# A hybrid decoder step on one core: GpSimd in written order, GpSimd roundings in the first products, later squares, and ACT copies that empty two PSUM banks ahead of the norm

## The chip, the cores and the metric

One core of one Trainium2 chip. The metric is the device time of one execution in microseconds (us); lower is better.

## The reference

One inference step of a one-layer decoder over 560 tokens: 16 meta tokens, 512 prompt tokens and 8 running sequences with 4 new tokens each. All arithmetic is fp32.

```python
def swiglu(x, w_gate, w_up, w_down):
    return (jax.nn.silu(x @ w_gate) * (x @ w_up)) @ w_down

x = x + 0.5 * swiglu(rmsnorm(x, g_ff1), w_ff1_gate, w_ff1_up, w_ff1_down)   # 1024 -> 2816 -> 1024
# mixer on rmsnorm(x, g_mix): q, k, v, o, two gates (4 heads x 128), and two 512-channel inputs
#   mLSTM: chunked, with state C (128 x 128), n, m of each head
#   RG-LRU: causal conv of width 4, block-diagonal gates (8 blocks of 64), linear recurrence h = a h + b
x = x + concat(mlstm_heads, lru_channels) @ w_out                           # 1024 -> 1024
x = x + 0.5 * swiglu(rmsnorm(x, g_ff2), w_ff2_gate, w_ff2_up, w_ff2_down)
y = rmsnorm(x, g_final)
```

(The order of the steps is abridged.) Outputs are y, the states C, n, m of the mLSTM, h of the RG-LRU, and the last conv inputs, for the prompt and for each of the 8 sequences.

## The kernel before

Everything is transposed: channels lie on the 128 partitions, tokens along the free dimension. x is eight tiles of 128 x 560 (`X`), the FFN's hidden size 22 tiles. TensorE (PE) gets fp32 accuracy by pieces: each operand is split into a rounded part `hi` and a remainder `lo`, and a product is the sum of hi·hi, hi·lo and lo·hi (`split_mm`, L296), each in two halves of 280 tokens (272 where the meta tokens are left out). Of weights, ACT rounds `whi` (L259) and VectorE (DVE) subtracts `wlo` (L264), units of 128 x 512 at a time, through rotating buffers of six, running ahead of their use by `AHEAD = 8, 6, 5, 4` units for load, sums, hi and lo. Part of the FFN runs as seven products in place of eight (`product7`, L409; sums of weight blocks are made by DVE in `s`).

PSUM has three double banks (`mm_tile`) and two single ones (`aux_tile`). A product must wait for a bank, so what reads a bank last (an evacuation by DVE or ACT) can hold PE.

The order of the work is written down as lists of short tokens, a step's name and its index. `FF1` and `FF2` are the plain part of the two FFNs, `MID1` and `MID2` the end of their down products mixed with the next norm, `PLAN` is the mixer. The code issues each step's instructions in this order, inside a region in which the engines of `MANUAL` run them as written: PE, ACT and DVE. GpSimd (POOL) and the DMA queue of SP are outside of this set, and a planner orders them by when their inputs come and by their place in the program. The mixer's preamble (`ident`, `cmask`, `smask`, `seqm`, `keep`, `RW`, `ones_r`, L890 to L919, all GpSimd) stands ahead of the region, and the planner places it.

Names that come up below:

- Start of FF1 (L636 to L695): `warm` is 20 matmuls on ones; `wh`, `wl` round and subtract the first weights (both on DVE, L664 and L662); `x`, `l` (`xa xb la lb` for the halves of tile 0) do it for x times the norm's gain (ACT L675, DVE L673); `p` is one 128-channel part of the first gate product (`p0k`) or up product (`p1k`); `s` squares a tile of x on ACT (L687), `a` adds it to `acc` on DVE (L690); `ga`, `gb` are two parts of the next gate product, `pn` the sum of `acc` over the partitions on PE (`psn`, L391), `rs nw` the root, `eg eu` scale a gate or up product by the norm (L544), `u`, `g` are products.
- MID1: `qa` to `qg` are the seven down products of a tile, `ia` to `ig` add them to X (L483).
- PLAN: `v k q x y o` with an index are products of 48 matmuls, `ev ek eq ex` their evacuations. `rg` (`do_wrg`) builds the block-diagonal gate weights: GpSimd memset L925, DMA L927, GpSimd cast L929 and subtraction L930. `g` (`do_g`) is the product for the mLSTM gates; ahead of it GpSimd copies columns of lo into the hi tile (L969), PE then reads them (`pgate`, L972). `ge gf gq ga gb gc gd gp` work on the gates' rows. For an RG-LRU tile `ex` puts the conv's input together (L1115 to L1117), `a` runs the gate matmuls (`prg`, L1145), `cc` makes the coefficients (L1175 on), `cd` sets the sequences' old state (GpSimd L1188), scans (DVE L1190) and copies the last states to `osm` (GpSimd L1191, L1192). For a head, `tk` and `tv` transpose k and v (`pt`, L1297), GpSimd copying a tail first (L1294); `sd` makes GpSimd's sums `D` (L1407 to L1411), `qw` q times weights for the sequences (GpSimd L1418, L1420), `n` the numerator and denominator (`pn`, L1430 to L1454), `cp` the new C states: GpSimd scales the old one by eight instructions (L1512), DVE adds (L1520).
- Tail (L783 to L860): `scale` multiplies the final norm into X and writes y; `state` and `state_out` make the last three heads' prompt states (PE L817, L818; ACT L821, L822).

```python
MANUAL = {mybir.EngineType.PE, mybir.EngineType.Activation, mybir.EngineType.DVE}
PLAN = """
rg1
v0 gn gs0 gs1 g gr0 gr1 ev0 rg0
...
v2 ev2 cd1 hd1 a2 ta2 ca2 b2 cb2 vm1 sk1 qw1 tb2 n1 cc2 cn1 hk2 ce0
```

Of the kernel before, what the change touches and what calls it, by code (L numbers as in the profile page):

```python
# [139 lines left out]
def hymba_step(ctx, tc, xT, wgu1, wdn1, win, wout, wgu2, wdn2, consts, small, c0t, wrg,  # L140
# [507 lines left out]
    for d, w in enumerate((None, (1, 0), (0, 1), (1, 1), (0, 2), (1, 2), None, None)):  # L648
        if d:
            nc.sync.dma_start(X[:, d, :], xT[d])  # L650
        if w:
# [81 lines left out]
    with tc.tile_pool(name="hp2", bufs=1) as hp, tc.tile_pool(name="sp2", bufs=1) as sp:  # L733
# [79 lines left out]
        def state(i):  # L813
            (k, v), t = keys[i], tails[i]
            py = st[:, 129 * i:129 * i + 129]
            for j in range(4):
# [1 line left out]
            pe.matmul(py, t[:, :P], t[:, P:], start=False, stop=True)  # L818
# [4 lines left out]

        fs = range(c0, c1)
        with tc.manual_schedule(engines=MANUAL | {mybir.EngineType.Pool}):
            for d in range(TAIL, KD):
# [33 lines left out]
            nc.scalar.dma_start(o_small[:, O_NP:O_NP + LATER], osm[:, O_NP:O_NP + LATER])  # L860
# [3 lines left out]
def mixer(ctx, tc, e):  # L864
# [318 lines left out]
    @step
    def do_cd(ct):
# [3 lines left out]
        pool.tensor_copy(ti[:, 528:584].rearrange("p (b j) -> p b j", j=7)[:, :, 2], C[:, H0 + 8 * ct:H0 + 8 * ct + 8])  # L1188
# [225 lines left out]
    def do_qw(h):  # L1414
# [5 lines left out]
        pool.tensor_tensor(qn, qw, n0.unsqueeze(2).to_broadcast([P, NB, 4]), op=ALU.mult)  # L1420

    @step
    def do_n(h):
# [29 lines left out]
        pe.matmul(pn[:, 1, 64:96], one_m[1][:32, :], W[:32, WO[5]:WO[5] + 32], start=True, stop=False)  # L1453
# [210 lines left out]
```

## Time and profile before

| | before |
|---|---|
| median of 3 runs | 1024.83 us (1024.37 to 1026.25) |
| profiled execution, its own time | 1024.98 us |
| its span | 1023.3 us |
| PE busy | 1010.1 us (99%) |
| DVE, ACT, POOL busy | 831.6, 558.3, 119.8 us |
| DMA | 102.85 MB, 101 GB/s on the mean |

How to read it: a busy share is of the whole span. Rows of the timeline give start, duration, engine, line, operation, tile out<-in, shape and count; in brackets stands the idle time of the engine before, and what ended it. `x48` means that so many instructions are put together in one row. Rows of the waits are: who waited, for whom, us in total, times, longest. Rows of the chain (start, duration, engine, tile, line) follow the work that ended last. PEld is PE's loading of weights, PEclk the clock that PE was granted (1.00 is full).

### The profile page before, as it was taken

To read this page: it belongs to the slowest core of one execution; us is meant where nothing else is said; L and a number is where in the kernel's file an instruction comes from. 1 tells how busy PE (TensorE), PEld (TensorE's weight loads), DVE (VectorE), ACT (ScalarE), POOL (GpSimd) and SP (SyncE) were. 2 spreads that over 40 slices of the span, in tenths; PEclk is the share of its full clock that TensorE was granted. 3 is DMA by queue.
4 is the path that set the end of the run, shared out by engine and by line. 5 is a ranking of instruction groups with operands and counts; after the bars stand their busy time and mean duration, and the time that the engine had idled before them with its cause. 6 is when DMAs were issued, how large, how long until landed. Compare 5 with 4: busy or idle time off the path is not lost.

```text
span 1023.3 us, 20215 instructions
## 1 busy us (share of the span) xinstructions
PE 1010.1 (99%) x7786; PEld 995.2 (97%) x7786; DVE 831.6 (81%) x1462; ACT 558.3 (55%) x1071; POOL 119.8 (12%) x198
## 2 busy tenths in 40 slices
PE   9999999999999999998999999999999999999998
PEld 8999999999999999998999999999999999999997
DVE  7988788888788797879888865799888899859774
ACT  6544555565544455475756743554555665654543
POOL 0000000000000035353651202100000000000002
PEclk9999999999999999998999999999999999999999
DMA  6222223223332334234142133223323323235222
GB/s 227 95 83 88 99 94 112 85 98 109 89 104 60 102 103 146 86 95 138 54 135 97 62 104 107 73 63 103 109 89 103 104 94 114 93 102 157 78 71 96
DMA packets 60985, 102.85 MB, mean 101 GB/s; under 512 B 8512, under 2 KB 16976, under 8 KB 60888
## 3 DMA queue, kind: packets, MB, share of 16 engines
q1 hardware_dynamic: 60200, 101.23, 30.8%
q8 instruction: 61, 1.00, 0.4%
q10 hardware_dynamic: 688, 0.32, 0.1%
q14 instruction: 36, 0.29, 0.1%
HBM read 95.20 MB, written 6.33 MB: 99 GB/s over the span
## 4 chain that ended last, share of the span: by engine, by line
PE 86%; DVE 7%; issue 2%; ACT 2%; POOL 2%; DMA 1%; SPq 0%; DVEq 0%; ACTq 0%; POOLq 0%
PE pb L409 27%; PE pad L409 20%; PE pd L296 15%; PE po L296 6%; PE pg L296 3%; PE pu L296 3%; PE pv L296 2%; PE py L296 2%; PE pq L296 2%; DVE wlo L264 2%; PE pd L792 1%; POOL c L1512 1%; PE px L296 1%; PE p L296 1%; PE pk L296 1%
## 5 line engine op out<-in xcount | busy, mean ns | idle before, releaser
L259 ACT CAST whi<-raw 128x512 fp32r<-128x512 f32 (+2 forms) x289 | 172.4, 606 | 160.7 <-PE pad L409 41.6
L264 DVE TENSOR_TENSOR wlo<-raw,whi 128x512 fp32r<-128x512 f32 (+2 forms) x289 | 197.2, 699 | 68.2 <-ACT whi L259 65.4
L259 ACT CAST whi<-s 128x512 fp32r<-128x512 f32 x180 | 111.8, 622 | 106.2 <-PE pb L409 36.4
L264 DVE TENSOR_TENSOR wlo<-s,whi 128x512 fp32r<-128x512 f32 x180 | 124.3, 692 | 12.6 <-ACT whi L259 6.5
L409 PE MATMUL pad<-q21h,whi 128*128 128x280 f32 (+1 forms) x360 | 104.2, 290 | 0.9 <-DVE X L483 0.9
L409 PE MATMUL pb<-qt4l,whi 128*128 128x280 f32 (+1 forms) x360 | 104.0, 289 | 0.0
L409 PE MATMUL pad<-q21l,whi 128*128 128x280 f32 (+1 forms) x360 | 104.0, 289 | 0.0
L409 PE MATMUL pad<-q21h,wlo 128*128 128x280 f32 (+1 forms) x360 | 104.0, 289 | 0.0
L409 PE MATMUL pb<-qt4h,whi 128*128 128x280 f32 (+1 forms) x360 | 103.9, 289 | 0.0
L409 PE MATMUL pb<-qt4h,wlo 128*128 128x280 f32 (+1 forms) x360 | 103.9, 289 | 0.0
L409 PEld LDWEIGHTS pad<-q21h,whi 128*128 128x128 f32 x360 | 67.8, 188 | 1.1 <-ACT whi L259 1.1
L409 PEld LDWEIGHTS pb<-qt4h,whi 128*128 128x128 f32 x360 | 67.9, 189 | 0.0
L409 PEld LDWEIGHTS pb<-qt4h,wlo 128*128 128x128 f32 x360 | 67.8, 188 | 0.0
L409 PEld LDWEIGHTS pb<-qt4l,whi 128*128 128x128 f32 x360 | 67.8, 188 | 0.0
L409 PEld LDWEIGHTS pad<-q21l,whi 128*128 128x128 f32 x360 | 67.8, 188 | 0.0
L409 PEld LDWEIGHTS pad<-q21h,wlo 128*128 128x128 f32 x360 | 67.8, 188 | 0.0
L239 DVE TENSOR_TENSOR s<-raw 128x512 f32<-128x512 f32 x90 | 61.5, 684 | 1.8 <-DMA raw<-in_wdn 1.8
L296 PE MATMUL pd<-hh,whi 128*128 128x280 f32 (+1 forms) x294 | 61.3, 290 | 0.6 <-ACT whi L259 0.4
L296 PE MATMUL pd<-hl,whi 128*128 128x280 f32 (+1 forms) x294 | 61.4, 290 | 0.2 <-DVE hl L557 0.2
L296 PE MATMUL pd<-hh,wlo 128*128 128x280 f32 (+1 forms) x294 | 61.2, 289 | 0.0
L378 POOL TENSOR_TENSOR acc<-acc,sq 128x560 f32<-128x560 f32 (+1 forms) x6 | 9.4, 1564 | 419.8 <-ACT sq L377 419.7
L409 PE MATMUL pb<-q11h,whi 128*128 128x280 f32 (+1 forms) x180 | 52.4, 291 | 0.0
(466 smaller groups left out, 2993.9 us busy)
## 6 DMA issues: line engine op xcount, KB each, us to landing
raw<-in_wgu SPq DMA_DIRECT2D x174, 256.0 KB, 2.7
raw<-in_wdn SPq DMA_DIRECT2D x71, 256.0 KB, 2.7
raw<-in_win SPq DMA_DIRECT2D x50, 256.0 KB, 3.3
raw<-in_wout SPq DMA_DIRECT2D x16, 256.0 KB, 3.1
raw<-in_wdn SPq DMA_DIRECT2D x18, 192.0 KB, 2.3
c<-in_c0t SPq DMA_DIRECT2D x4, 512.0 KB
out_o_cs<-c SPq DMA_DIRECT2D x4, 512.0 KB, 3.0
X<-in_xT SPq DMA_DIRECT2D x7, 280.0 KB, 5.0
```

The costliest lines, as they stand in the source:

```text
L239: dve.tensor_tensor(q[k], q[x], q[y], op=op)
L259: act.copy(ready[i][0][:, :src.shape[-1]], src)
L264: dve.tensor_tensor(lo, src, hi, op=ALU.subtract)
L296: state["mm"] = pe.matmul(ps[:, hf, :n], a[:, ws], b[k][:, c0 + hf * n:c0 + hf * n + n], start=first and j == 0 and i == 0, stop=last and ...
L378: (dve if d == KD - 1 else pool).tensor_tensor(self.acc[:, c0:], self.acc[:, c0:], s[:, c0:], op=ALU.add)
L409: pe.matmul(ps, a[:, k * P:k * P + P], b, start=first and k == 0 and i == 0, stop=k == KD // 2 - 1 and i == 2, skip_group_check=not first)
L792: pe.matmul(pd[d - TAIL][:, hf, :b - a], u[:, o:o + P], v[:, C16 + a:C16 + b], start=f == c0 and m == 0, stop=f == c1 - 1 and m == 2)
L1512: pool.tensor_scalar(c0[:, b, :], c0[:, b, :], Wb[:, b, 3:4], None, op0=ALU.mult)
```

## The change

It has six parts.

- GpSimd joins `MANUAL`: its instructions in the regions run as written.
- FF1's start: the constants' first DMA goes from SP's queue to ACT's; the order of loads changes; all roundings `wh` but the first go to GpSimd; `p00` is done by halves (`pa pb`); squares and their adds come later; `ga` takes four tiles instead of three; two ACT copies (`co`) empty the banks of the first two products ahead of the norm, and `eg0 eu0` then scale in SBUF; the weights of `w3` are prepared earlier.
- MID1: `ib3 if3` ahead of `qe3`.
- Mixer: some tokens change place; `cw` (the scaling of the old C) is a step of its own right after `n`; `cc1` is split into `ci1` and `cj1`; several small operations move from GpSimd to DVE (the sum of Wi, xp's memset and copy, a0's and V's memsets, the th copy of `cd`), and `E`'s minimum from DVE to GpSimd; `om` is copied and written in `gq`; `qw` gets a third GpSimd operation that adds a row of W to `qn`, and `n` drops the matmul L1453.
- FF2: for f = 2 the up product's evacuation and pieces run by halves; `rd3` ahead of `yb3`, `rd5` ahead of `d7`.
- Tail: each of the three states has its own bank, and is copied out and written by itself; GpSimd scales two tiles in place of one.

```diff
-MANUAL = {mybir.EngineType.PE, mybir.EngineType.Activation, mybir.EngineType.DVE}
+MANUAL = {mybir.EngineType.Pool, mybir.EngineType.PE, mybir.EngineType.Activation, mybir.EngineType.DVE}
 PLAN = """
 rg1
 v0 gn gs0 gs1 g gr0 gr1 ev0 rg0
...
-q0 ek0 gd ge
-k1 gf L0 eq0 ex0 cx0 gp hq0 hk0 ek1 gq hx0 tv0
+q0 ek0 gd
+k1 eq0 gf ge L0 ex0 cx0 tv0 gp ek1 hq0 hk0 gq hx0
...
-k2 ca1 cb1 ek2 cc1 tv1 am1
-x2 f0 cv1 p0 ex2 cf0 tk1 cp0 cx2 ck1
+k2 ca1 cb1 ek2 ci1 tv1 am1
+x2 f0 cv1 p0 ex2 cf0 tk1 ck1 cp0 cj1 cx2
...
-v2 ev2 cd1 hd1 a2 ta2 ca2 b2 cb2 vm1 sk1 qw1 tb2 n1 cc2 cn1 hk2 ce0
+v2 ev2 cd1 hd1 a2 ta2 ca2 b2 cb2 vm1 sk1 qw1 tb2 n1 cw1 cc2 cn1 hk2 ce0
...
 FF1 = """
-warm wh00 xa0 la0 wl00 xb0 lb0 p00 x1 wh10 wl10 l1 p10 p01 s0 p11 x2 l2 wh01 wl01 s1 p02 x3 l3 wh11 p03 wl11 p12 p13 a1 s2
-x4 wh02 l4 wl02 p04 s3 x5 l5 p05 wh12 wl12 p14 p15 a2 s4 x6 l6 p06 p16 a3 x7 l7 p07 p17 s5 a4 w0 s6 s7 a5 w1 a6 a7 ga1 pn
-w2 rs0 nw0 rs1 nw1 eg0 sg0 ...
+warm wh00 xa0 la0 wl00 xb0 pa0 lb0 pb0 wh10 wl10 p10 x1 l1 p01 p11 x2 l2 wh01 wl01 p02 wh11 wl11 x3 l3 p12 p03 p13 s0
+x4 l4 wh02 wl02 p04 wh12 wl12 x5 l5 p14 p05 p15 s1 x6 l6 p06 p16 s2 x7 l7 p07 p17 s3 a1 w0 s4 a2 s5 a3 w1 s6 a4 s7 co0 co1 a5 a6 a7 ga1 pn
+w2 w3 rs0 nw0 rs1 nw1 eg0 sg0 ...
...
 FF2 = """
-em2 Bh2 Eh2 hh2 hl2 Bl2 tc2 El2 td2 Fh2 d0 ya3 rd0 Ah3 d2 Fl2 Al3 rd2 d3 d4 yb3 d5 Bh3 rd3 rd4 ta3 d1 Bl3 d7 tb3
-rd5 tc3 Eh3 d6 td3 rd1 El3 Fh3 rd6 Fl3 rd7
+ei2 Bh2 Eh2 hi2 hj2 Bl2 tc2 El2 td2 Fh2 d0 ya3 rd0 Ah3 d2 Fl2 Al3 rd2 d3 d4 rd3 yb3 d5 Bh3 rd4 ta3 d1 Bl3 rd5 d7 tb3
+tc3 Eh3 d6 td3 rd1 El3 Fh3 rd6 Fl3 rd7
...
 MID1
-... nq2 nq6 qe3 ib3 if3 ie3 ...
+... nq2 nq6 ib3 if3 qe3 ie3 ...
...
+    act.dma_start(C[:, :8], consts[:, :8])
     act.activation(dum, eps_c, AF.Identity)
...
-            split_mm(ps["g", f], range(3), nrm.hi, nrm.lo, c0, last=False, w=[z["w"]])
+            split_mm(ps["g", f], range(KD // 2), nrm.hi, nrm.lo, c0, last=False, w=[z["w"]])
...
+        def out(j):
+            what = "gu"[j]
+            z[what, 0] = z_tile()[:, c0:]
+            act.copy(halves(z[what, 0], n), start[j][:, :, :n])
...
-                dve.tensor_copy(h[:, o], src)
+                (pool if j or p else dve).tensor_copy(h[:, o], src)
...
     def do_cd(ct):
...
-        pool.tensor_copy(ti[:, 528:584]..., C[:, H0 + 8 * ct:H0 + 8 * ct + 8])
+        dve.tensor_copy(ti[:, 528:584]..., C[:, H0 + 8 * ct:H0 + 8 * ct + 8])
...
         pool.tensor_tensor(qn, qw, n0.unsqueeze(2).to_broadcast([P, NB, 4]), op=ALU.mult)
+        qs = qn.rearrange("p b j -> p (b j)")[:32]
+        pool.tensor_tensor(qs, qs, d["W"][:32, WO[5]:WO[5] + 32], op=ALU.add)
...
-        pe.matmul(pn[:, 1, 64:96], one_m[1][:32, :], W[:32, WO[5]:WO[5] + 32], start=True, stop=False)
-        pe.matmul(pn[:, 1, 64:96], one_m[1], d["qn"].rearrange("p b j -> p (b j)"), start=False, stop=True)
+        pe.matmul(pn[:, 1, 64:96], one_m[1], d["qn"].rearrange("p b j -> p (b j)"), start=True, stop=True)
...
     @step
+    def do_cw(h):
+        c0, Wb = D[h]["c0"], D[h]["Wb"]
+        for b in range(NB):
+            pool.tensor_scalar(c0[:, b, :], c0[:, b, :], Wb[:, b, 3:4], None, op0=ALU.mult)
...
         def state(i):
-            py = st[:, 129 * i:129 * i + 129]
+            py = st[i] = mm_tile("st")[:, 0, :129]
...
+            state_out(0)
             scale(a, b, pool, 7, 8, nc.scalar)
-            for d0, d1 in ((0, 1), (1, 3), (3, 5), (5, 7)):
+            state_out(1)
+            scale(a, b, pool, 6, 7, nc.scalar)
+            for d0, d1 in ((0, 1), (1, 3), (3, 5), (5, 6)):
                 scale(a, b, dve, d0, d1, nc.sync)
-            for i in range(LATER):
-                state_out(i)
-            nc.scalar.dma_start(o_cp[0:LATER].rearrange("h p e -> p h e"), cp)
-            nc.scalar.dma_start(o_small[:, O_NP:O_NP + LATER], osm[:, O_NP:O_NP + LATER])
+            state_out(2)
+            nc.sync.dma_start(o_small[:, O_NP:O_NP + LATER], osm[:, O_NP:O_NP + LATER])
```

More of the change, by code (lines that the diff above doesn't have):

```diff
@@ L49 @@
 q3 cv2 ek3 hx3 eq3 p1 s2 tk2 cp1 cd2 ck2
-v3 qw2 m2 vm2 L3 a3 sd2 hd2 ev3 n2 ta3 ca3 b3 hk3 cb3 cn2 tv3 tb3 cc3 sk2 am3 cd3
+v3 qw2 m2 vm2 L3 a3 sd2 hd2 ev3 n2 cw2 ta3 ca3 b3 hk3 cb3 cn2 tv3 tb3 cc3 sk2 am3 cd3
 o0 p2 hq3 cv3 ce2 ce3 cl2 cl3 cm2 w3 cp2 eo0
@@ L53 @@
 o1 eo1 mo0 s3 my0 m3 f2 sd3
-y1 tk3 cf2 to1 hd3 ey1 gy1 ck3 so0 mo1 n3 sk3 cn3 cm3
+y1 tk3 cf2 to1 hd3 ey1 gy1 ck3 so0 mo1 n3 cw3 sk3 cn3 cm3
 y2 ey2 so1 f3
@@ L77 @@
 FF1 = """
-warm wh00 xa0 la0 wl00 xb0 lb0 p00 x1 wh10 wl10 l1 p10 p01 s0 p11 x2 l2 wh01 wl01 s1 p02 x3 l3 wh11 p03 wl11 p12 p13 a1 s2
-x4 wh02 l4 wl02 p04 s3 x5 l5 p05 wh12 wl12 p14 p15 a2 s4 x6 l6 p06 p16 a3 x7 l7 p07 p17 s5 a4 w0 s6 s7 a5 w1 a6 a7 ga1 pn
-w2 rs0 nw0 rs1 nw1 eg0 sg0 ya0 yb0 Ah0 Bh0 Al0 eu0 ta0 gb1 tb0 mu0 Eh0 Bl0 tc0 td0 eg1 Fh0 Fl0 El0 ya1 yb1 hh0 Ah1 u1 sg1 Bh1 hl0 Al1 eu1 g2 mu1 u2 ta1 Bl1 tb1 hh1 eg2 eu2 tc1 sg2 mu2 hl1 g3 td1 hh2 hl2 eg3 Eh1 sg3 Fh1 El1 mg3 u3 ya2 em3 Ah2 hh3 Fl1 hl3 yb2 d4 Al2 ta2 Bh2 Bl2 tb2 tc2 rd4 d0 d2 Eh2 rd0 td2 Fh2 El2 d6 Fl2 ya3 yb3 rd6 Ah3 Bh3 Bl3 d5 rd2 Al3 ta3 d3 tb3 rd5 d1 Eh3 v2 tc3 El3 td3 Fh3 d7 rd1 v3 Fl3 rd7 rd3
+warm wh00 xa0 la0 wl00 xb0 pa0 lb0 pb0 wh10 wl10 p10 x1 l1 p01 p11 x2 l2 wh01 wl01 p02 wh11 wl11 x3 l3 p12 p03 p13 s0
+x4 l4 wh02 wl02 p04 wh12 wl12 x5 l5 p14 p05 p15 s1 x6 l6 p06 p16 s2 x7 l7 p07 p17 s3 a1 w0 s4 a2 s5 a3 w1 s6 a4 s7 co0 co1 a5 a6 a7 ga1 pn
+w2 w3 rs0 nw0 rs1 nw1 eg0 sg0 ya0 yb0 Ah0 Bh0 Al0 eu0 ta0 gb1 tb0 mu0 Eh0 Bl0 tc0 td0 eg1 Fh0 Fl0 El0 ya1 yb1 hh0 Ah1 u1 sg1 Bh1 hl0 Al1 eu1 g2 mu1 u2 ta1 Bl1 tb1 hh1 eg2 eu2 tc1 sg2 mu2 hl1 g3 td1 hh2 hl2 eg3 Eh1 sg3 Fh1 El1 mg3 u3 ya2 em3 Ah2 hh3 Fl1 hl3 yb2 d4 Al2 ta2 Bh2 Bl2 tb2 tc2 rd4 d0 d2 Eh2 rd0 td2 Fh2 El2 d6 Fl2 ya3 yb3 rd6 Ah3 Bh3 Bl3 d5 rd2 Al3 ta3 d3 tb3 rd5 d1 Eh3 v2 tc3 El3 td3 Fh3 d7 rd1 v3 Fl3 rd7 rd3
 """.split()
@@ L109 @@
 ie1 qf1 id1 ns0 d6 ns1 qa2 e7 ia2 qb2 qc2 rd6 ig1 qd2 ib2 ic2 if2 qa3 ia3 qe2 ie2 qg2 qf2 ig2 re7 qb3 id2 nq1 qc3
-ic3 qd3 nq2 nq6 qe3 ib3 if3 ie3 nq5 qg3 ns5 nq4 ns2 qf3 id3 t7 ns4 ig3 nq3 ns6 ns3 rt7 ns7 nq7
+ic3 qd3 nq2 nq6 ib3 if3 qe3 ie3 nq5 qg3 ns5 nq4 ns2 qf3 id3 t7 ns4 ig3 nq3 ns6 ns3 rt7 ns7 nq7
 """.split()
@@ L538, in em, with ei, hi, hj @@
             tt(halves(z["u", f], n), ps["u", f][:, :, :n], halves(z["g", f], n), op=ALU.mult)
+        def ei(f):
+            z["u", f] = z_tile()[:, c0:]
+            for hf in range(2):
+                o = slice(hf * n, hf * n + n)
+                tt(z["u", f][:, o], ps["u", f][:, hf, :n], z["g", f][:, o], op=ALU.mult)
+        def hi(f):
+            for hf in range(2):
+                o = slice(hf * n, hf * n + n)
+                act.copy(h[f][0][:, c0 + hf * n:c0 + hf * n + n], z["u", f][:, o])
+        def hj(f):
+            for hf in range(2):
+                o, q = slice(hf * n, hf * n + n), slice(c0 + hf * n, c0 + hf * n + n)
+                tt(h[f][1][:, q], z["u", f][:, o], h[f][0][:, q], op=ALU.subtract)
         def scaled(what):
             def fn(f):
+                if (what, f) in z:
+                    tt(z[what, f], z[what, f], r[:, c0:], op=ALU.mult)
+                    return
                 z[what, f] = z_tile()[:, c0:]
-                src = ps[what, f] if (what, f) in ps else start["gu".index(what)]
-                tt(halves(z[what, f], n), src[:, :, :n], halves(r[:, c0:], n), op=ALU.mult)
-            return fn
+                tt(halves(z[what, f], n), ps[what, f][:, :, :n], halves(r[:, c0:], n), op=ALU.mult)
+            return fn
+        def out(j):
+            what = "gu"[j]
+            z[what, 0] = z_tile()[:, c0:]
+            act.copy(halves(z[what, 0], n), start[j][:, :, :n])
         def sg(f):
@@ L607, in rd @@
             return fn
-        steps.update(ga=first_part, gb=second_part, mg=mg, em=em, g=product("g"), u=product("u"), pn=nrm.mean, rs=nrm.table, nw=nrm.step, eg=scaled("g"), eu=scaled("u"), sg=sg, mu=mu,
+        steps.update(ga=first_part, gb=second_part, mg=mg, em=em, co=out, ei=ei, hi=hi, hj=hj, g=product("g"), u=product("u"), pn=nrm.mean, rs=nrm.table, nw=nrm.step, eg=scaled("g"), eu=scaled("u"), sg=sg, mu=mu,
                      hh=hh, hl=hl, ya=y(0), yb=y(1), ta=ta, tb=tb, tc=tc_, td=td, d=dn("d", *plain), rd=rd("d"), v=run_ahead)
@@ L635, in hymba_step @@
     n1.open()
-    nc.sync.dma_start(C[:, :8], consts[:, :8])
     w0, wt = [[raw_tile(), raw_tile()] for _ in range(2)], [[hl_tile(), hl_tile()] for _ in range(2)]
@@ L647, in hymba_step @@
     nc.sync.dma_start(X[:, 0, Q:], xT[0, :, Q:])
[L648 to L651, printed above, removed]
+    load_w(1, 0)
+    for d, *ws in ((1,), (2, (0, 1), (1, 1)), (3,), (4, (0, 2)), (5, (1, 2)), (6,), (7,)):
+        nc.sync.dma_start(X[:, d, :], xT[d])
+        for w in ws:
             load_w(*w)
@@ L676, in start_x, with start_p @@
         return fn
-    def start_p(j, d):
+    def start_p(j, d, hfs=(0, 1)):
         p = start.setdefault(j, None)
@@ L682, in start_p @@
         t = wt[j][d // 4]
-        split_mm(p, [d], n1.hi, n1.lo, 0, d == 0, d == KD - 1, w=[[u[:, d % 4 * P:] for u in t]])
+        split_mm(p, [d], n1.hi, n1.lo, 0, d == 0, d == KD - 1, hfs, w=[[u[:, d % 4 * P:] for u in t]])
     def start_sq(d):
@@ L698, in hymba_step @@
                   xa=start_x(0, Q, 0), la=start_x(0, Q, 1), xb=start_x(Q, T, 0), lb=start_x(Q, T, 1), p=start_p,
+                  pa=lambda d: start_p(0, d, (0,)), pb=lambda d: start_p(0, d, (1,)),
                   s=start_sq, a=start_add, w=up_to)
@@ L820, in state_out @@
         def state_out(i):
-            act.copy(cp[:, i, :], st[:, 129 * i:129 * i + P])
-            act.copy(osm[:, O_NP + i:O_NP + i + 1], st[:, 129 * i + P:129 * i + P + 1])
+            act.copy(cp[:, i, :], st[i][:, :P])
+            act.copy(osm[:, O_NP + i:O_NP + i + 1], st[i][:, P:])
+            nc.scalar.dma_start(o_cp[i], cp[:, i, :])
         fs = range(c0, c1)
@@ L849, in hymba_step @@
             root(1)
-            st = aux_tile("st")
+            st = {}
             cp = tmp("cp")[:, :LATER * P].rearrange("p (a b) -> p a b", b=P)
@@ L1032, in do_ge @@
         Wi, E = mp.tile([H, NB, 4], F32, name="Wi"), row("E")
-        pool.tensor_tensor(Wi, blk4(A[:, NP:T]), m0.unsqueeze(2).to_broadcast([H, NB, 4]), op=ALU.add)
+        dve.tensor_tensor(Wi, blk4(A[:, NP:T]), m0.unsqueeze(2).to_broadcast([H, NB, 4]), op=ALU.add)
         act.activation(E, mrow, AF.Exp, scale=-1.0)
         act.activation(Wi, Wi, AF.Exp)
-        dve.tensor_scalar(E, E, 1e17, None, op0=ALU.min)
+        pool.tensor_scalar(E, E, 1e17, None, op0=ALU.min)
         act.activation(E, E, AF.Square, scale=EPS ** 0.5)
@@ L1092, in do_gq @@
                           seqm.unsqueeze(1).to_broadcast([96, H, NB]), op=ALU.mult)
+        mrow = G["m"]
+        pool.tensor_copy(om[:, 0:1], mrow[:, NP - 1:NP])
+        pool.tensor_copy(om[:, 1:9], seq(mrow, 3))
+        nc.sync.dma_start(e["o_m"], om)
     def bias(i, j, h):
@@ L1111, in do_ex @@
         xp = L[ct]["xp"] = slot("xp")
-        pool.memset(xp[:, 0:3], 0.0)
-        pool.tensor_copy(smp(xp, 0, 3),
+        dve.memset(xp[:, 0:3], 0.0)
+        dve.tensor_copy(smp(xp, 0, 3),
                          C[:, CS + 24 * ct:CS + 24 * ct + 24].rearrange("p (b j) -> p b j", j=3))
@@ L1171, in do_cc, with do_ci @@
     @step
-    def do_cc(ct):
+    def do_ci(ct):
         l = L[ct]
-        tr, ti, a0, tt, xc = l["th", 0], l["th", 1], l["a0"], l["tt"], l["xc"]
+        a0, tt = l["a0"], l["tt"]
         dve.tensor_scalar(a0, a0, 0.5, 0.5, op0=ALU.mult, op1=ALU.add)
@@ L1177, in do_cc, with do_cj @@
         dve.scalar_tensor_tensor(a0, tt, 2.0, a0, op0=ALU.subtract, op1=ALU.mult)
+    @step
+    def do_cj(ct):
+        l = L[ct]
+        tr, ti, a0, xc = l["th", 0], l["th", 1], l["a0"], l["xc"]
         dve.tensor_tensor(tr, tr, a0, op=ALU.mult)
@@ L1180, in do_cc @@
         dve.tensor_scalar(a0, a0, -2.0, -1.0, op0=ALU.mult, op1=ALU.add)
-        pool.memset(a0[:, 528:584].rearrange("p (b j) -> p b j", j=7)[:, :, 2], 0.0)
+        dve.memset(a0[:, 528:584].rearrange("p (b j) -> p b j", j=7)[:, :, 2], 0.0)
+    @step
+    def do_cc(ct):
+        do_ci(ct)
+        do_cj(ct)
     @step
@@ L1310, in do_cv @@
         v5w = mp.tile([96, P], F32, tag="v5w", name="v5w", bufs=1)
-        pool.memset(V[:, :, 128:129], 1.0)
+        dve.memset(V[:, :, 128:129], 1.0)
         act.activation(v5w, pt[:96, 1, 128:256], AF.Identity, scale=wst[:96, 5, h:h + 1])
@@ L1506, in do_cp @@
     @step
+    def do_cw(h):
+        c0, Wb = D[h]["c0"], D[h]["Wb"]
+        for b in range(NB):
+            pool.tensor_scalar(c0[:, b, :], c0[:, b, :], Wb[:, b, 3:4], None, op0=ALU.mult)
+    @step
     def do_cp(h):
@@ L1510, in do_cp @@
         px, py = ps["p", h]
-        for b in range(NB):
-            pool.tensor_scalar(c0[:, b, :], c0[:, b, :], Wb[:, b, 3:4], None, op0=ALU.mult)
         pn = mp.tile([P, 9], F32, tag="cpn", name="cpn", bufs=2)
```

8 lines of the change are left out of this document (2 added, 6 removed).

## The prediction

> **What bounds the kernel now.** I read the page's busy times first, then the waits, then the windows for stages that the change touches.
>
> ```profile
> span 1023.3 us, 20215 instructions
> PE 1010.1 (99%) x7786; PEld 995.2 (97%) x7786; DVE 831.6 (81%) x1462; ACT 558.3 (55%) x1071; POOL 119.8 (12%) x198
> L264 DVE TENSOR_TENSOR wlo<-raw,whi 128x512 fp32r<-128x512 f32 (+2 forms) x289 | 197.2, 699 | 68.2 <-ACT whi L259 65.4
> PE pt L1297 <- DVE xp L1117: 4.0, 1, 4.0
> PE pad L409 <- DVE X L483: 0.9, 1, 0.9
> DVE hs L1190 <- POOL th L1188: 6.3, 4, 4.5
> PE pq L296 <- DVE kT L955: 0.3, 1, 0.3
> PE pl L1209 <- DVE c L1520: 0.3, 1, 0.3
> ```
>
> PE is busy for 1010.1 of 1023.3 us, so only 13.2 us of idle time can be won, besides matmuls removed or run at a low clock. GpSimd (POOL) has 12% of work: its load can't bound anything, its order can. The waits name two PE stalls that the change aims at (columns: us in total, times, longest), 4.0 us at `pt` in the mixer and 0.9 at `pad` in MID1, and one behind them: VectorE's scan waited 4.5 us for a tiny GpSimd copy. The profiled execution took 1024.98, 0.15 above the median of 1024.83; the sum is made against it.
>
> **The start.** Windows (length, then busy time of PE, PEld, DVE, ACT, POOL, then clock, DMA share, GB/s) and timeline rows:
>
> ```profile
> 5.36:20.63 15.27, 14.15 (x98) 13.07 (x98) 13.04 (x24) 12.99 (x20) 0.00 (x0) 1.00 0.81 281
> 20.63:35.24 14.61, 14.38 (x104) 13.48 (x103) 12.58 (x23) 6.54 (x11) 0.00 (x0) 1.00 0.27 88
> 5.36 1.20 PE L296 MATMUL p<-xh,whi 128*128 128x280 f32 x2
> 21.43 1.51 DVE L690 TENSOR_TENSOR acc<-acc,sq 128x560 f32<-128x560 f32 x2
> 22.99 1.21 PE L391 MATMUL psn<-acc,ones 128*128 128x280 f32 x4
> 35.24 6.19 PE pg L296 x48
> 395.25 0.67 POOL L929 CAST wrgh<-wrg 128x512 fp32r<-128x512 f32 x1 [2.35 <-DMA wrg<-in_wrg]
> ```
>
> A product is 48 matmuls in 6.19 us (the chain's row at 35.24), 0.129 each. The first two are 96 of them, 12.4 us, but take 15.27, with VectorE busy for 13.04. The change takes five weight roundings off VectorE (three of 128x256, two of 128x512) and puts them on an empty GpSimd; the 0.67 row is its price for 128x512, and half of that for 128x256 makes 2.4 us in all, beside other work. The first matmul stays at 5.36, behind the warm-up matmuls, which aren't changed; the constants' DMA, moved from SP's queue to ACT's, lets SP's loads begin one issue (some 0.45) earlier and costs ACT an issue before its first rounding, neither of which that start waits for. With VectorE relieved, the earlier loads and the norm's squares after the roundings, the products are limited by the arrival of x and weights: 12.4 and some 1.2 of waits, end near 19.0. `ga` has 24 matmuls now (3.1 us), so the norm's sum comes at about 22.2 (VectorE's last adds, 0.75 each, end at 21.3 to 22.8) where `psn` stood at 22.99. Behind it follow `psn` 0.62, `gb` 24 matmuls 3.1, `u1` 6.2, and 0.4 to 1.0 of waits: end at 32.5 to 33.1, where `g2` began at 35.24. The two ACT copies that empty the banks (12.99 busy before 20.63, 6.54 in the next 14.6) fit in ACT's idle time. VectorE is at 12.58 of 14.61 there and can give back up to 0.5 later. Taken: **−2.1**; bounds 0 (VectorE no faster) and −2.7.
>
> [...]
>
> **MID1: `ib3 if3` ahead of `qe3`.**
>
> ```profile
> 373.06 2.37 DVE L264 TENSOR_TENSOR wlo<-raw,whi 128x512 fp32r<-128x512 f32 x2
> 373.50 3.15 POOL L378 TENSOR_TENSOR acc<-acc,z 128x560 f32<-128x560 f32 x2 [1.27 <-ACT z L377]
> 375.35 0.79 DVE L483 SCALAR_TENSOR_TENSOR X<-pad,X 128x280 f32<-128x280 f32 x2
> 395.37 0.45 DVE L330 SCALAR_TENSOR_TENSOR rn<-psn,r 128x280 f32<-128x280 f32 x1
> ```
>
> PE waits for the bank that L483 reads; that read stands behind two weight subtractions of 2.37 us. Put ahead of them, it frees the bank before PE asks. **−1.0** (the 0.9 wait and its edges; bounds 0 and −1.1).
>
> **GpSimd in written order: the gate product `g`.** GpSimd's rows and the first matmul of `g`:
>
> ```profile
> 382.64 0.98 POOL L969 CAST whi<-wlo 128x160 fp32r<-128x160 f32 x2 [2.23 <-DVE wlo L264]
> 386.10:391.40 5.30, 5.30 (x41) 5.13 (x40) 4.69 (x7) 1.87 (x4) 5.15 (x19) 1.00 0.81 277
> 391.43 0.51 POOL L925 MEMSET wrg<- 128x512 f32 x1
> 396.01 1.45 POOL L930 TENSOR_TENSOR wrgl<-wrg,wrgh 128x512 fp32r<-128x512 f32 x1
> 391.98 0.63 PE L972 MATMUL pgate<-xh,whi 128*128 128x280 f32 x2
> ```
>
> Today the planner lets L969's two copies, which `pgate` reads, run at 382.64, ahead of everything of the mixer. In the order of PLAN, `rg1` is the first token and `g` the sixth. With GpSimd among the engines in written order, L969 stands behind `rg1`'s memset, its cast, which waits for a DMA behind that memset, and its subtraction. That memset came at 391.43, behind the mixer's preamble (5.15 us of GpSimd from 386.10), the cast at 395.25, the subtraction ended at 397.46, and a copy takes 0.49 and some 0.1 to be seen: 398.1 instead of 383.6. PE is ready at 391.98: **a wait of 6.1**. Behind PE in order stand `x0` and everything else. What a wait of this size does to the clock is shown by the mixer's 4.0:
>
> ```profile
> 468.50:472.80 4.30, 0.29 (x3) 0.11 (x3) 4.25 (x10) 0.00 (x0) 0.35 (x3) 0.74 0.22 68
> 472.80:477.00 4.20, 4.20 (x20) 4.11 (x21) 3.37 (x6) 2.12 (x6) 0.78 (x2) 0.50 0.63 201
> 477.00:481.50 4.50, 4.50 (x36) 4.50 (x36) 4.36 (x7) 2.98 (x6) 0.00 (x0) 0.96 0.29 117
> ```
>
> 4.2 us at 0.50 and 4.5 at 0.96 lose 2.1 + 0.2. A 6.1 wait costs this too: 6.1 + 2.1 = **+8.2**. Bounds: 0, if the copies still come first; +2.2, if the memset goes ahead of the preamble (it needs a buffer that GpSimd's own work frees at 386.1): 386.6 memset, cast after DMA and preamble at 391.9, subtraction to 394.1, no clock loss. I take the upper end, because the preamble and the memset start at nearly the same moment and the preamble is earlier in the program.
>
> **The mixer.**
>
> ```profile
> 461.20:490.30 29.10, 25.09 (x179) 24.35 (x177) 26.29 (x41) 15.56 (x35) 11.23 (x20) 0.88 0.39 128
> 461.18 1.38 DVE L1190 TENSOR_TENSOR_SCAN hs<-a,th 128x584 f32<-128x584 f32 x1 [4.52 <-POOL th L1188]
> 487.03 0.69 POOL L1418 TENSOR_TENSOR qw<-qT,Wb 128x32 f32<-128x32 f32 x1
> 490.32 0.74 DVE L953 TENSOR_TENSOR vT<-pv,r 128x560 f32<-128x560 f32 x1 [1.14 <-PE pv L296]
> 492.88 1.53 DVE L1190 TENSOR_TENSOR_SCAN hs<-a,th 128x584 f32<-128x584 f32 x1 [1.15 <-POOL th L1188]
> 496.59 0.40 POOL L1191 COPY osm<-hs 128x1 f32<-128x1 f32 x1
> 491.87 0.34 PE pn L1430 x4
> 497.20 0.24 PE pn L1453 x2
> ```
>
> The copy L1188 goes to VectorE, so the 4.52 us wait at 461.18 is gone, VectorE is some 4.3 us earlier, and the `pt` wait falls to about 0.4: −3.6, and −2.2 with the clock. But `qw1`, at 487.03 today, is written behind `cd1`, whose GpSimd copies L1191 follow the scan, and that follows `ev2` (the 490.32 row). Counted from the end of `v2`: `ev2` 0.15 + 0.74, L1187 0.76, th copy 0.2, scan 1.45, the copies 0.4, then `qw1`'s three small operations, of which the first two are the last that matmuls before L1454 can cover: at least 4.05. PE is ready for `n1` 1.59 after `v2` (`prg`, 490.28 to 491.87): a wait of 2.45 or more. VectorE has 26.29 us of work in the 29.1 up to 490.3, and 0.5 more from GpSimd; with 4.3 of advance and 1.9 of waits left it brings `n1` to start at about 490.3, after some 4.1 of PE idle that takes with 6 chances in 10 the clock loss of 2.1. `n1` then ends at 497.1, where 497.6 was (L1453 at 497.20, then L1454): **−0.5** for the whole stretch (−3.4 if `n1`'s wait is 2.45 at full clock, +0.7 if both are worst). So most of the advance is given back in a new wait of the same size, 20 us later. [...]
>
> Dropping L1453 (its 0.24 and the gap to the next row's start, −0.31 each) in `n2 n3` gives −0.6; in `n0` and `n1` it lies inside a wait or is counted already. The GpSimd sum that replaces it (some 0.5) is inside the 4.05. `ek1` earlier and the new order of `cw`, `cp`: −0.6, the two waits for `kT` and `pl` at 0.3 each. The split of `cc1` takes half of its VectorE chain from ahead of `tv1` to behind `cp0`, where VectorE is 4.3 ahead: 0. The small memsets, Wi's sum, `E`'s minimum and the copies of `om` with their DMA, now issued from `gq` instead of `ge`, feed no matmul within several products (6.2 us each): 0, and SP's queue, past which that DMA moves, holds only weights four to eight units ahead. Mixer: −0.5 −0.6 −0.6 = **−1.7**.
>
> **FF2.**
>
> ```profile
> 694.70 1.35 DVE L505 SCALAR_TENSOR_TENSOR X<-pd,X 128x544 f32<-128x544 f32 x2
> 695.56 0.49 PE L296 MATMUL pd<-hh,whi 128*128 128x272 f32 x2 [0.43 <-ACT whi L259]
> ```
>
> PE stands about 0.6 before 695.56, for a weight prepared behind `yb3`'s sums and `rd3`; `rd3` ahead of `yb3`, `rd5` ahead of `d7` and `f=2` by halves: **−0.8** (0 to −1.0).
>
> **The tail.**
>
> ```profile
> 1018.50 0.48 PE L818 MATMUL st<-kv 16*128 16x129 f32 x2
> 1020.27 0.49 ACTq L860 DMA_DIRECT2D out_o_small<-osm  x1
> out_o_cp<-cp SPq DMA_DIRECT2D x1, 64.0 KB, 2.6
> ```
>
> All three states are copied out after the last matmul (1018.50), and the last DMA is issued at 1020.27. With a bank for each, only one copy and a 64 KB DMA remain; the last issue comes at about 1019.4 (−0.9), but is followed by a transfer of this size, 2.6 to land, where a small one stood; I give 0.3 back: **−0.6** (−1.2 to +0.2).
>
> **Sum:** −2.1 −1.0 +8.2 −1.7 −0.8 −0.6 = +2.0: 1027.0 by the profiled execution, 1026.8 for the median.
>
> **Rivals.** *B, the memset goes ahead of the preamble:* `g` waits 2.2, and 1026.8 − 6.0 = 1020.8. For it: L969 itself overtook the preamble at 382.64. Against: its buffer is free only at 386.1. *C, the written order leaves L969 where it was* (the change doesn't do there what its flag says, or the weights of `rg1` land early enough): 1026.8 − 8.2 = 1018.6. For it: the copies ended at 383.6, 8.4 us before PE needed them, so their inputs allow it. *D, slower: GpSimd's roundings hold VectorE's two-input steps in the first 20 us:* the start's −2.1 is lost, 1028.9; it decides once VectorE loses over 2 us before 21.4. For it: the pair at 373.06 takes 1.2 each beside GpSimd's two-input sum at 373.50, where the group's mean is 0.70 (the L264 row at the top); against: the 0.45 beside the cast, and casts have one input.
>
> **How the numbers follow.** A measurement of this kernel tells about 0.2% (2.0 us) from no change: faster is under 1022.8, slower over 1026.9. My forecast has 0.60, with its own range 1023.5 to 1029 from the bounds of `n1` and the start; it lies at the edge, so 0.06 of that is faster, 0.30 the same, 0.24 slower. B 0.13 (0.12 faster, 0.01 same), C 0.19 (all faster), D 0.08 (slower). Together 0.37, 0.31, 0.32. The range from 1017.0 to 1030.0 leaves out half of C below and little of D above.
>
> **What would show it.** Start: `psn` near 22.2 and `g2` near 33. MID1: no PE wait at `pad`. `g`: PE waits for GpSimd L969 by some 6 us, and a clock of 0.50 in the 4 us behind it. Mixer: no wait at `pt`, a new one of 2.5 to 4 at `n1` for `qn`. If `pgate` follows `psn` without a gap, the forecast is wrong by 8, and the change is faster.

## The result and the profile after

The changed kernel is slower: 1039.2 us (median of 6, 1034.86 to 1042.61) against 1025.07, ratio 1.0134 with a 95% interval of 1.01 to 1.0168. Its six times fall into two groups, 1034.9 to 1036.3 at a mean granted clock of 0.993 and 1042.1 to 1042.6 at 0.984; the profiled execution is one of the first (1034.86, span 1033.1), so its time is 9.9 above that of the profile before. I forecast 1026.8 and 1017 to 1030.

The page's first lines and the PE rows of the waits (who waited, for whom, us, times, longest):

```profile
span 1033.1 us, 20223 instructions
PE 1010.7 (98%) x7778; PEld 996.0 (96%) x7778; DVE 834.4 (81%) x1479; ACT 559.9 (54%) x1074; POOL 126.1 (12%) x188
```

```profile
PE pn L1468 <- POOL qw L1454: 6.2, 1, 6.2
PE pgate L997 <- POOL whi L994: 5.2, 1, 5.2
PE pt L1335 <- POOL t L1330: 2.2, 1, 2.2
PE pv L296 <- DVE xl L368: 1.1, 1, 1.1
PE pl L1245 <- DVE c L1561: 0.8, 1, 0.8
PE pden L1476 <- ACT zh L1300: 0.7, 1, 0.7
```

PE has as much work as before and 9.2 us more of idle time. The `pt` wait of 4.0 for VectorE is gone; three new ones, 13.6 us together, all name GpSimd (POOL), which is busy for 12% of the span. L994 are the copies of `g` (L969 before), L1330 the copy of v's tail (L1294), L1454 is `qw` (L1418).

Where the time came from, by start times of the same matmuls in both traces (PE's lead or lag against before): −2.6 us at `g2` (35.08 before, 32.44 after); −3.7 behind MID1; −2.6 at the norm's `psn` (391.25, 388.61); +2.9 when `pgate` starts and +5.6 at `x0` behind it; +8.5 behind the wait at L1335, +7.5 at `px` of `x1`, +7.0 at the first `prg` and +6.7 behind `n0`; +0.7 at head 1's `pA`, since the old `pt` wait is gone; +7.1 when `n1` starts and +9.2 behind it; +10.5 at FF2; +9.8 at the end.

The windows show the clock (length, then busy time of PE, PEld, DVE, ACT, POOL, then clock, DMA share, GB/s), first of the changed kernel's profile, then of its other group, from the experiment `again`:

```profile
388.60:394.90 6.30, 1.12 (x6) 0.58 (x4) 3.98 (x7) 1.47 (x3) 3.19 (x8) 0.95 0.39 108
394.90:402.00 7.10, 7.07 (x33) 7.07 (x34) 2.69 (x3) 0.62 (x1) 2.83 (x4) 0.56 0.10 22
429.40:434.00 4.60, 4.58 (x35) 4.32 (x36) 3.45 (x8) 2.57 (x8) 3.00 (x7) 1.00 0.23 70
498.80:503.00 4.20, 4.20 (x11) 2.87 (x12) 3.99 (x7) 1.04 (x2) 4.11 (x4) 0.50 0.17 64
503.00:508.00 5.00, 5.00 (x31) 4.02 (x30) 0.11 (x2) 0.95 (x4) 3.67 (x7) 0.95 0.00 0
```

```profile
430.00:436.00 6.00, 6.00 (x36) 5.74 (x35) 5.11 (x10) 2.62 (x8) 2.47 (x5) 0.72 0.15 52
494.00:500.40 6.40, 0.25 (x2) 0.01 (x1) 6.33 (x11) 5.82 (x7) 2.83 (x4) 0.68 0.26 82
500.40:516.00 15.60, 15.55 (x52) 12.49 (x53) 6.06 (x11) 4.56 (x11) 7.79 (x10) 0.50 0.05 17
```

Both groups have the same waits. In the second one the clock is also low behind L1335 (0.72 where it was 1.00), and behind `n1` it stays at 0.50 for some 16 us in place of under 5. Lined up matmul by matmul, that is +1.5 and +5.2 us: nearly all of the 6.9 us between the two profiles.

GpSimd's rows for the three waits, in the changed kernel:

```profile
387.94 0.52 POOL L950 MEMSET wrg<- 128x512 f32 x1
392.35 0.61 POOL L954 CAST wrgh<-wrg 128x512 fp32r<-128x512 f32 x1 [2.93 <-DMA wrg<-in_wrg]
393.05 1.34 POOL L955 TENSOR_TENSOR wrgl<-wrg,wrgh 128x512 fp32r<-128x512 f32 x1
394.34 1.02 POOL L994 CAST whi<-wlo 128x160 fp32r<-128x160 f32 x2
427.27 1.61 POOL L1061 TENSOR_SCALAR E<-E 4x560 f32<-4x560 f32 x1 [6.00 <-ACT E L1059]
429.11 0.26 POOL L1330 COPY t<-vT 128x96 f32<-128x96 f32 x1
496.37 0.56 POOL L1227 COPY osm<-hs 128x1 f32<-128x1 f32 x1 [3.56 <-DVE hs L1226]
496.87 1.20 POOL L1228 COPY osm<-hs 128x8 f32<-128x8 f32 x1
498.04 0.69 POOL L1454 TENSOR_TENSOR qw<-qT,Wb 128x32 f32<-128x32 f32 x1
```

Each time the engine stands idle in front of something that nobody needs yet (a DMA, ACT's Exp, VectorE's scan), with the small operation that PE needs queued behind it.

### The profile page after: what moved, and what is told of

It is laid out like the page before. It is cut to its first block, busy times and chain, and to the rows that moved or that the text cites. A ratio compares the mean times of both kernels' runs of the same rounds, so it can differ in the third digit from the quotient of the medians.

```text
span 1033.1 us, 20223 instructions
## 1 busy us (share of the span) xinstructions
PE 1010.7 (98%) x7778; PEld 996.0 (96%) x7778; DVE 834.4 (81%) x1479; ACT 559.9 (54%) x1074; POOL 126.1 (12%) x188
## 4 chain that ended last, share of the span: by engine, by line
PE 88%; DVE 5%; ACT 2%; POOL 2%; issue 1%; DMA 1%; SPq 0%; DVEq 0%; POOLq 0%; ACTq 0%
PE pb L410 26%; PE pad L410 20%; PE pd L296 15%; PE po L296 6%; PE pu L296 4%; PE pg L296 4%; PE px L296 2%; PE pk L296 2%; PE pq L296 2%; PE py L296 1%; PE p L296 1%; DVE wlo L264 1%; PE pd L815 1%; PE pn L1472 1%; PE pgate L997 1%
```

## The experiments

Theory: the loss is the written order of GpSimd at three places, and the half clock behind the waits. Rival: the mixer's moves lose by themselves.

**The changed kernel again.**

> The changed kernel once more, unchanged, since its six times fell into two groups (1034.9 to 1036.3 and 1042.1 to 1042.6, mean clock 0.993 and 0.984). Theory 1 (a wait of 2 to 3 us, such as the one at pt L1335, halves the clock in some executions and not in others): both groups again, and a profile of the upper group shows one or more extra stretches at 0.50 behind that wait, worth some 7 us together. Theory 2 (the groups belong to chips): all runs of this call in one group.

1041.75 (1041.66 to 1042.81), ratio 1.0171 (1.0156 to 1.0187): all in the upper group here, while the first six, of the same kernel, had both. Its profile gave the second block of windows above. So the extra time is half clock behind the same waits, as theory 1 had it. All four runs on this chip agree, which fits theory 2 too; `qw1_first` below, on the same chip, spreads over 10 us, so the chip isn't all of it.

**`rg1` behind `g`.**

```diff
-rg1
-v0 gn gs0 gs1 g gr0 gr1 ev0 rg0
+v0 gn gs0 gs1 g rg1 gr0 gr1 ev0 rg0
```

> One edit: the token rg1 goes behind g. Theory 1 (g's two GpSimd copies wait in written order behind rg1's memset, DMA, cast and subtraction): the 5.2 us wait at pgate and the clock loss behind it go, 8.2 in all, so 1026.7 where the changed kernel has 1034.9. Rival (the copies wait for the preamble on GpSimd, rg1 or not): a wait of 1 to 2 us stays without clock loss, 1028 to 1029. Rival (planner puts them late for another reason): no change.

1036.72, 5.0 less than `again`; the 1026.7 expected was counted from the lower group, and this run has the slow clock of the upper one. No wait at `pgate` is left, and PE is 7.8 ahead of `again` at `x0`: the term is what was expected. Then some 3 are given back: 0.7 since the wait at L1335 (here L1334) grows, 1.1 by more slow clock behind it than in `again`, and 1.5 by a clock of 0.50 from 581.99 to 585.40, where `again` has 1.00. Its longest waits:

```profile
PE pn L1467 <- POOL qw L1453: 6.2, 1, 6.2
PE pt L1334 <- POOL t L1329: 2.8, 1, 2.8
PE pv L295 <- DVE xl L367: 1.5, 1, 1.5
```

**`qw1` first in its row.**

```diff
-v2 ev2 cd1 hd1 a2 ta2 ca2 b2 cb2 vm1 sk1 qw1 tb2 n1 cw1 cc2 cn1 hk2 ce0
+v2 qw1 ev2 cd1 hd1 a2 ta2 ca2 b2 cb2 vm1 sk1 tb2 n1 cw1 cc2 cn1 hk2 ce0
```

> One edit: the token qw1 goes from behind sk1 to the front of its row, ahead of ev2 and cd1. Theory 1 (qw stands in written order behind the copies that wait for VectorE's scan): the 6.2 us wait at n1 and the 2.4 lost behind it go but for about 1 us in which GpSimd ends its sums D: 7 to 8 less than the changed kernel, 1027 to 1028. Rival (n1 would wait as long for D or for VectorE anyway): the wait moves to pden or another line of n1 and less than 3 us are won.

1030.58 (1028.52 to 1038.27). The 6.2 wait shrinks to 1.6, for `qn`; in the profiled execution (1029.1) `n1` starts 4.6 earlier against the changed kernel and 2.3 more are won inside it, 7.0 in all, as expected. The upper runs have a lower clock (down to 0.985); where in them it was low no trace shows, so the wait of 1.6 may still bring the half clock.

**E's minimum back on VectorE.**

```diff
-        pool.tensor_scalar(E, E, 1e17, None, op0=ALU.min)
+        dve.tensor_scalar(E, E, 1e17, None, op0=ALU.min)
```

> One edit: the minimum of E goes back from GpSimd to VectorE. Theory 1 (the copy t for tv0 stands behind this minimum, which waits for ACT): the 2.2 us wait at pt L1335 goes, some 1.4 of which is given back until n0, so 1.3 to 1.5 less, 1033.5; and if this wait is what splits the runs in two groups, all runs are in the lower group. Rival (the groups come from another wait): the two groups stay, both 1.4 lower.

1042.08: nothing won, and the groups not settled either. The wait at L1335 is still 2.1. VectorE's rows tell why:

```profile
426.22 0.44 DVE L1061 TENSOR_SCALAR E<-E 4x560 f32<-4x560 f32 x1 [3.04 <-ACT E L1059]
427.36 0.17 DVE L1143 TENSOR_TENSOR xp<-px,r 128x32 f32<-128x32 f32 x1
```

The minimum waits for ACT's Exp wherever it stands; now VectorE waits 3.04, `xp` is late, GpSimd's copies of `xp` and the copy `t` behind them too. My reading of that wait was wrong: not the engine but the place of `ge`, ahead of `tv0`, makes it.

**All three places moved.**

```diff
-k1 eq0 gf ge L0 ex0 cx0 tv0 gp ek1 hq0 hk0 gq hx0
+k1 eq0 gf ex0 cx0 tv0 ge L0 gp ek1 hq0 hk0 gq hx0
```

together with the moves of `rg1` and `qw1`.

> The changed kernel with three moves of tokens: rg1 behind g, qw1 to the front of its row, and ge L0 behind tv0, since with E's minimum on VectorE the same wait went through VectorE (its 3.0 us for ACT's Exp of ge). Theory 1 (what the change loses are three waits that come from GpSimd's written order, and the half clock behind them): no wait of PE over 2 us in the mixer, clock 1.00 there, and 1034.9 - 8.2 (g) - 7 (n1, as qw1_first showed) - 1.5 (pt L1335) = 1018.2, in one group. Rival (the mixer's engines are late anyway, and the waits only move to the next place): over 1022, with new waits of PE behind the old ones.

1021.92 (12 runs, 1018.62 to 1027.94), ratio 0.9976 (0.9958 to 0.9994): 17 us less than the changed kernel. The four runs nearest to full clock (0.999 and 1.0) have 1018.6 to 1018.9, as expected; the rest lie in several groups up to 1027.9 at 0.989, so the part on one group was wrong. In the profiled execution (1024.1) a PE wait of 1.5 for `qn` is left at `n1`, and behind it:

```profile
482.70:484.40 1.70, 0.21 (x2) 0.00 (x0) 1.70 (x4) 1.26 (x2) 1.54 (x4) 1.00 0.14 40
484.40:496.00 11.60, 11.56 (x40) 9.03 (x41) 8.71 (x14) 7.43 (x13) 9.07 (x11) 0.56 0.18 63
```

**The parts outside the mixer alone**, put on the kernel before: FF1's start, MID1, FF2 and tail, with GpSimd left to the planner.

> The kernel before with only the parts of the change that lie outside the mixer: start of FF1, MID1, FF2 and tail; GpSimd stays with the planner. Theory 1 (these parts give what the offsets of the two traces show): start -2.6, MID1 -1.0 with 1.1 given back at v0, FF2 -0.5, tail -0.1, in all -3.1: 1021.4 where before has 1024.5. Rival (the start is good only with GpSimd in written order, since the planner would place its roundings late): the start gains nothing, 1024.

1023.34, ratio 0.9988 (0.998 to 0.9997): a gain of 1.2 where 3.1 were expected. The start (−2.5 at `g2`) and MID1 (−1.0) are in the trace, but 1.5 are lost in `v0`, which now waits for x's pieces (`pv` for `xl`), and 0.8 and 0.6 in two more places of the mixer where PE waits for VectorE. The start's gain is there without the written order.

**The changed kernel with GpSimd left to the planner** (`MANUAL` as before, all else changed).

> The changed kernel without GpSimd among the engines in written order (one edit, MANUAL as before). Theory 1 (the written order is what loses): no wait at pgate or n1 for GpSimd, 1017 to 1020, in one group. Rival (the moved steps and operations of the mixer lose by themselves, whoever orders GpSimd): over 1028.

1022.63 (1018.31 to 1024.05), ratio 0.9974 (0.9961 to 0.9987). One word in a set is worth 16 us between the medians, and the moved steps don't lose by themselves. The median is above the 1017 to 1020 expected, and the ten runs form no one group (1018.3 at a clock of 0.999 to 1024.1 at 0.993). No wait for GpSimd in the mixer is left; the longest is at `n1` again:

```profile
PE pn L1468 <- DVE vT L978: 1.9, 1, 1.9
```

**The kernel before with GpSimd in written order, and nothing else.**

> The kernel before with only GpSimd added to MANUAL. Theory 1: g's copies wait behind rg1 as in the changed kernel, 8 us with the clock, and the copies of cd1 and qw1 stand in written order too, so 1033 to 1042, and two groups can come. Rival (the wait at g needs the other moves): under 1028.

1053.01, ratio 1.0279 (1.0263 to 1.0295): more than either theory gave. Four waits:

```profile
PE pt L1299 <- POOL t L1294: 5.4, 1, 5.4
PE pl L1209 <- DVE c L1520: 5.1, 1, 5.1
PE pgate L972 <- POOL whi L969: 5.1, 1, 5.1
PE pn L1430 <- POOL qw L1418: 4.6, 1, 4.6
```

So the changed kernel's other moves repair two of these, leave `pgate` and `n1`, and add the one at L1335. What repairs them is read from the rows and not tested one by one: the copy `t` for which `pt` waits here stands behind a0's memset, which waits 6.95 for VectorE (the change gives it to VectorE), and GpSimd's scaling of C, 6.6 long, stands right ahead of the sum in `c` for which `pl` waits (`cw` as a step of its own takes it from there).

**`qw1` a row earlier, and the scan behind `n1`.** Both on top of `waits_out`, with the tail's last small DMA on ACT's queue; the second also moves `cj1 cd1`.

```diff
-q2 L2 s1 w1 m1 sd1 eq2 hx2 hq2
-v2 qw1 ev2 cd1 hd1 a2 ta2 ca2 b2 cb2 vm1 sk1 tb2 n1 cw1 cc2 cn1 hk2 ce0
+q2 L2 s1 w1 m1 qw1 sd1 eq2 hx2 hq2
+v2 ev2 cd1 hd1 a2 ta2 ca2 b2 cb2 vm1 sk1 tb2 n1 cw1 cc2 cn1 hk2 ce0
... and for the second, with cj1 taken from its row:
+v2 ev2 hd1 a2 ta2 ca2 b2 cb2 vm1 sk1 tb2 n1 cw1 cj1 cd1 cc2 cn1 hk2 ce0
```

> As waits_out, but qw1 stands one row earlier, ahead of GpSimd's sums D (sd1), and the tail's last small DMA goes back to ACT's queue. Theory 1 (n1 there waits for two things that end within 0.3 us of each other, GpSimd's qn and VectorE's vT behind the half of cc1 that the change moved there): the wait at n1 names VectorE and is still 1.0 to 1.9 us, the runs still fall into groups from 1018 to 1027. Tail: the last DMA issues about 0.5 us sooner after the last matmul. Rival (qn alone is late): no wait over 0.5 at n1, one group near 1017.

> As qw1_early, and cj1 and cd1 go behind n1, so that VectorE has 2.0 us less work ahead of vT and some 5 less ahead of n1's operands. Theory 1 (the halved clock behind n1 is started by PE's wait ahead of it, even one of 1.5 us, since n1's small matmuls behind it keep PE from looking busy): no wait over 0.5 us at n1, no stretch at 0.50 there, all runs in one group near 1016.5. Rival (n1's small matmuls halve the clock by themselves): no wait at n1, and still groups with 0.50 stretches behind it, 1017 to 1025.

`qw1_early` has 1024.78 (1020.02 to 1028.74), ratio 0.9997: the wait at `n1` is still 1.7 (the trace names nobody for it), and the clock of its runs goes from 1.0 to 0.989. `late_scan` has 1020.81 (1019.67 to 1023.52), ratio 0.9968 (0.9957 to 0.9979): 0.3% below the kernel before and well below the changed one. Its wait at `n1` is 0.6, its runs lie at 0.996 to 1.0. Two of its waits, and two windows, the first up to `n1` and the second over it:

```profile
PE pn L1467 <- DVE vT L977: 0.6, 1, 0.6
PE pv L1519 <- DVE sql L1510: 1.4, 1, 1.4
```

```profile
480.00:484.20 4.20, 3.62 (x28) 3.38 (x26) 4.20 (x6) 2.15 (x4) 2.75 (x4) 1.00 0.05 15
484.20:492.00 7.80, 7.76 (x47) 6.26 (x48) 7.51 (x13) 7.51 (x13) 7.27 (x4) 1.00 0.27 98
```

It is 4 us above the expected 1016.5, in part since VectorE's late work makes a new wait of 1.4 at `pv`. Against `qw1_early`'s profile, where the clock is as high, PE is 1.9 ahead at `n1` and 0.4 behind from the next `pl` on: what the median wins is clock alone. The spread fell from 8.7 to 3.9 us with the wait, so theory 1 is borne out in direction. The rival isn't excluded: two runs still have 0.996, 1023.4 and 1023.5 lie in its range, and no such run was profiled. A wait of 1.7 left the clock at 1.00 in `qw1_early`'s profile, so the wait's length alone doesn't settle it. That `n1`'s small matmuls keep PE from looking busy was my guess, which no run shows.

## Why the prediction was wrong

**Start (−2.1), right:** `g2` starts 2.6 earlier; `psn` came at 22.11 for 22.2 forecast. Rival D, GpSimd's roundings holding up VectorE, didn't come about. What got longer where the two engines run side by side is the roundings:

```profile
5.08 0.40 POOL L686 CAST whi<-raw 128x256 fp32r<-128x256 f32 x1 [3.62 <-DMA raw<-in_wgu]
7.33 1.65 DVE L695 SCALAR_TENSOR_TENSOR xl<-X,C,xh 128x560 fp32r<-128x560 f32 x2 [1.20 <-ACT xh L697]
7.61 1.64 POOL L686 CAST whi<-raw 128x256 fp32r<-128x256 f32 x2 [2.13 <-DMA raw<-in_wgu]
```

A rounding of 128x256 takes 0.40 at 5.08 and 0.82 each beside VectorE's remainders, which keep their 0.8 each (0.80 in the kernel before); all five take 3.6, where I had 2.4. The row at 395.37 that I set against D was weak evidence: one step of 128x280, where the remainders here are 128x560.

**MID1 (−1.0), right on the spot, and half forgotten:** the wait at `pad` is gone, −1.0. What is late next was not asked: PE reached `v0` earlier than the pieces of x, and a wait of 1.1 there (`pv` for `xl`) took it all back at once.

**The gate product (+8.2), right:** 5.6 of delay at `pgate` for 6.1, and 2.6 of slow clock for 2.1. That the two misses cancel to the same 8.2 is luck; the mechanism is not, for `rg_behind_g` shows that it is the written order. This one step, read off the order of the tokens and GpSimd's rows, is the largest in the change.

**The mixer (−1.7), wrong, and this is the step that failed;** the traces give +4.9 there. The new wait at `n1` was sized too small, and the new place of `ge` was put at nothing. Three terms:

- `n1` (−0.5 for the stretch, measured +2.5). The old wait went as forecast: −6.0 with the clock, for −5.8. The new one is 6.2 long instead of 4.1. I took 0.4 for GpSimd's two copies ahead of `qw`, and 0.15 between the end of `v2` and `ev2`. The rows give 1.67 for the copies (496.37 to 498.04), where the trace before had a second one of 0.64 (below, first row) that I left out: 1.3 of the 2.1. The rest is VectorE: `ev2` came only at 493.29, 2.5 behind the end of `v2`. Ahead of it stand the 2.0 us of `cj1`, which the change moved there from ahead of `tv1` and which I put down at 0 because VectorE was "4.3 ahead". `late_scan`, with `cj1` behind `n1`, shows what they cost there: `ev2` 1.9 earlier than in `qw1_early` (483.46 for 485.35). What they would have cost in the old place no run shows:

```profile
496.93 0.64 POOL L1192 COPY osm<-hs 128x8 f32<-128x8 f32 x1
482.04 0.76 DVE L1210 SCALAR_TENSOR_TENSOR th<-th,xc 128x584 f32<-128x584 f32 x1
493.29 0.73 DVE L978 TENSOR_TENSOR vT<-pv,r 128x560 f32<-128x560 f32 x1
494.93 1.38 DVE L1226 TENSOR_TENSOR_SCAN hs<-a,th 128x584 f32<-128x584 f32 x1
```

- E's minimum and the new place of `ge` (0, measured +2.0: +2.9 behind the wait at L1335, of which 0.9 are `tv0`'s own matmuls, which stand earlier in the row now). "Feed no matmul within several products" was true of their results and missed what stands behind them on GpSimd: `tv0`'s copy. `e_on_dve` shows that it isn't the engine of the minimum; with `ge` behind `tv0` (`waits_out`, two other moves beside it) the wait falls from 2.2 to 0.5. I had asked that question at `g` and `n1` only.
- Dropped matmuls and small waits (−0.6 and −0.6, measured +1.3 behind `n1`): L1453's drop gives 0.24 each time and the wait for `kT` went (0.5 at `q1`), but `pl` waits 0.6 and `n3` 0.8 longer.

**The clock, wrong in kind:** I took one price, 2.1 to 2.2 for each long wait. The runs show that the same wait costs 2.4 or 7.6 behind `n1`, where PE has small matmuls, and nothing or 1.5 behind L1335. That puts the median of the six between the groups, 4.3 above the profiled execution. What the price lacked is the length of the low stretch, which isn't the same in each execution. Windows cut at the clock's changes, two of the changed kernel's profile and two of `again`:

```profile
394.26:401.09 6.83, 6.16 (x26) 6.16 (x27) 2.87 (x4) 0.62 (x1) 3.47 (x6) 0.50 0.10 23
496.66:503.49 6.83, 4.70 (x12) 3.22 (x13) 6.25 (x11) 3.15 (x4) 6.67 (x8) 0.50 0.11 40
431.39:434.81 3.42, 3.42 (x17) 3.42 (x16) 2.99 (x9) 1.55 (x5) 1.08 (x3) 0.50 0.21 82
496.25:516.73 20.48, 16.28 (x55) 13.22 (x56) 10.14 (x17) 8.66 (x15) 10.16 (x13) 0.50 0.10 38
```

In the changed kernel's profile the clock is 0.50 for 6.83 us at `pgate` and again for 6.83 at `n1`. In `again` it is so for 3.42 at L1335, where the first profile has 1.00, and for 20.48 at `n1`. Why the same wait of 6.2 at `n1` goes with 6.83 us in one execution and with 20.48 in another, no run shows. Waits shorter than the 4.0 from which I took the price were followed by 0.50 too: 2.1 in `again` (third row), 1.5 in `waits_out`.

**FF2 (−0.8), right:** −0.6, from +10.5 to +9.9. **Tail (−0.6), wrong and small:** −0.1, from +9.9 to +9.8. The last small DMA went to SP's queue, where it is issued only behind the eight writes of y:

```profile
1021.23 8.71 SPq L807 DMA_DIRECT2D out_y<-X  x8
1028.43 0.48 PE L841 MATMUL st<-kv 16*128 16x129 f32 x2
1029.28 0.34 ACTq L846 DMA_DIRECT2D out_o_cp<-cp  x1
1030.03 0.48 SPq L885 DMA_DIRECT2D out_o_small<-osm  x1
```

With it on ACT's queue (`qw1_early`) it is issued 1.3 behind the last `st` row instead of 1.6, yet the span ends 4.7 behind that row in both kernels: the issue didn't set the end. What does is open.

By profiled executions the sum is −2.6 −1.0 +1.0 +8.2 +4.9 −0.7 = +9.8, where I had +2.0 (−0.7 is FF2 and tail): 6.6 of the 7.8 between them lie in the mixer. The 4.3 from there to the median are the clock, for which the forecast had one price and no second group.
